# Mask sums, first taps, paired conditioning columns and free weight remainders in a two-layer diffusion step

## Chip, cores and metric

One core of one Trainium2 chip runs the whole program, one launch. The metric is device microseconds of a run, the median of the runs shown. PE is the matrix engine, DVE the vector engine, ACT the scalar engine, POOL the general engine, SP the queue that issues the transfers.

## What is computed

One step of a two-layer backbone over 128 prompt tokens and 512 sample tokens of width 2048. In each layer:

```python
h = rmsnorm(x, norm_pre[l]) * (1.0 + scale) + shift
(qa, ka, va, za, beta_raw, alpha_raw, cq, ckv, kpe, zb, xc, zc) = split_cols(h @ w_in[l])
oa, s_f, s_b = delta_branch(qa, ka, va, za, beta_raw, alpha_raw, conv_w[l], a_log[l],
                            dt_bias[l], o_norm_a[l], s0_f, s0_b)
ob = mla_attend(qn, qp, kn, kp, vb) * jax.nn.silu(zb)
oc = multiscale_pool(xc, w_pool[l], pool_scale[l]) * jax.nn.silu(zc)
y = jnp.concatenate([oa, ob, oc], axis=-1) @ w_out[l]
x = x + gate * rmsnorm(y, norm_post[l])
```

`scale`, `shift` and `gate` come from `silu(cond) @ w_ada[l] + b_ada[l]`, for two conditions. `delta_branch` has 8 heads: a convolution of 5 taps over q, k and v, then a gated delta rule in both directions, which needs `decay = exp(where(tri, gc_i - gc_j, -inf))` and the inverse of a triangular matrix for every block of 128 tokens.

## The kernel before

Layout. Tokens are five tiles of 128 (`NT`), held as two groups of 384 and 256 columns. A product in full precision is three products of rounded halves: `wsplit` (line 767) makes of four weight tiles a rounded half `hi` (a copy on ACT) and a remainder `lo` = raw - hi (a subtraction on POOL), each 128x512, into three buffers; `win_group` (line 783) multiplies them with the split activations, per weight tile three products over 384 and three over 256 columns. These are the projections of `w_in`; in the trace and the orders below they read `psum<-slabr`.

Order of the work. Nothing is issued in the order of the source. The class `Sched` records every operation, gives each a cost by `cost` (line 209), and `run` (line 350) plays engines, transfers and buffers forward; an operation goes to its engine when it is ready there, by priority (`later` shifts it). `either` (line 309) records an operation with a second form for another engine, and the engine that is idle first in this play takes it. `issue` (line 469) writes the result out, so each engine has a fixed order; line 499 issues everything, and all rows carry it. On the chip each engine follows its order, whatever the real times are.

Stages of a layer: `phase_a` makes the projections for gates and attention, the attention (`mla`), then for each of 8 heads `head_in` (projections of k, q, v and gate, with `conv_tile`, line 841) and `delta` (line 1182), then four pooling groups (`pool_group`); `phase_b` (line 1485) is the output projection. `head_in` of head h+1 is recorded ahead of `delta` of head h+1, so projections of the next heads and pooling groups stand between the small products of a scan and fill PE. In the first layer the conditioning columns of the second are worked in with `ada_cols` (line 1475): 16 beside the pooling groups, 16 beside the output projection.

A head, with the lines that the text speaks of:

- `conv_tile`: first tap `tensor_scalar` on DVE over 642 columns (line 849), four further taps on DVE (line 851).
- `delta`, lines 1188 to 1194: the decay table E, two directions of 128 x (5 x 128). A transfer fills it; per tile t one DVE step adds a per-partition scalar and the mask; one ACT exponential over 640 columns follows.
- key and query products, per tile three products over 256 columns from `kq` (hi and lo of k and q), into the one bank `pr`; four DVE steps multiply them with E (`slabV`/`slabW` as outputs) and free the bank for the next tile.
- the inversion: diagonal blocks go through DRAM into 40 rows, 31 pairs of DVE steps (`TENSOR_TENSOR slab<-slab 40x31` to `40x256` and back to `40x31`), a copy 40x1024, and through DRAM back.
- the scan: begins with 20 products 32x32 (`slab,slabW 32x32`) that need the landed inverse, then steps of 128x128 with DVE between them.

The DVE order mixes the inversion of head h+1 with the scan of head h.

`ada_cols`: a column block of 128 of `w_ada` (1 MB) lands in one of two buffers `ad2w`; 16 products into a bank, an ACT copy to `ao2`, a transpose into the same bank tag, a DVE reduction into `mcol`. `ad2w` lies over the buffers E, so it can be filled only when the last head has used them.

Of the kernel before, what the change touches and what calls it, by code (L numbers as in the profile page):

```python
# [18 lines left out]
NK = 16  # L19
# [4 lines left out]
NT = 5  # L24
# [477 lines left out]
class Body:  # L502
# [5 lines left out]
    def memory(self):  # L508
# [46 lines left out]
        put("S", SW - 128, [("ao2", 1, 128)], SW)  # L555
# [211 lines left out]
    def wsplit(self, raw, either=False):  # L767
        nc = self.nc
        n = cols(raw)
        hi = self.T("whi", [128, n], F32R)  # L770
        lo = self.T("wlo", [128, n], F32R)
        if either:
            self.copy(hi, raw)
            self.rest(lo, raw, hi)
        else:
            nc.scalar.activation(hi, raw, AF.Copy)
            nc.gpsimd.tensor_tensor(lo, raw, hi.bitcast(F32), op=ALU.subtract)
        return hi, lo
# [62 lines left out]
    def conv_tile(self, l, c0, ci, out):  # L841
# [7 lines left out]
        nc.vector.tensor_scalar(ac, cp[:, 0:KQW], w(0), None, op0=ALU.mult)  # L849
# [5 lines left out]
    def phase_a(self, l):  # L855
# [29 lines left out]
        for g in range(4):  # L885
            self.pool_group(l, g)
            if l == 0:
                self.ada_cols(l + 1, 16 + 4 * g, 20 + 4 * g, "ad2w", "pr2")
# [293 lines left out]
    def delta(self, l, h, ins):  # L1182
# [5 lines left out]
        for d in range(2):  # L1188
            e = self.T("E", [128, NT, 128])
            nc.sync.dma_start(e.rearrange("p t c -> p (t c)"), self.gcd[0].rearrange("(d h t) c -> d h (t c)", d=2, h=8)[d, h].partition_broadcast(128))  # L1190
            for t in range(NT):
                v.scalar_tensor_tensor(e[:, t], e[:, t], self.NGC[:, d * 8 + h, t:t + 1], self.mask[d], op0=ALU.add, op1=ALU.add)
            nc.scalar.activation(e, e, AF.Exp)
            E.append(e)
# [280 lines left out]
    def ada_cols(self, l, i0, i1, tag, pst):  # L1475
        nc, a = self.nc, self.a
        for i in range(i0, i1):
            w = self.T(tag, [128, NK, 128])
            nc.sync.dma_start(w, a["w_ada"][l, :, i * 128:(i + 1) * 128].rearrange("(k p) n -> p k n", p=128))
            p = self.ps(pst)  # L1480
            self.ada_rows(p, w, 0, True, True)
            with nc.later(-2):
                self.ada_sum(self.mcol[i // 16][:, :, i % 16:i % 16 + 1].rearrange("p v k -> p k v"), p, self.T("ao2", [128, 128]), pst)

    def phase_b(self, l):
# [53 lines left out]
        def columns(n):  # L1539
# [3 lines left out]
            for kc in range(NK // kn):  # L1543
# [6 lines left out]
                if n in (1, 2) and not last:  # L1550
                    i = 8 * (n - 1) + kc
                    self.ada_cols(l + 1, i, i + 1, "ad2w", "hp")
# [107 lines left out]
```

## Time and profile before

| | us |
|---|---|
| median of 3 runs | 2668.93 |
| lowest and highest run | 2667.51, 2675.01 |
| the profiled execution | 2681.82 |
| its span | 2680.0 |
| outside the span | 1.8 |

Engines by share of the span: PE 96%, DVE 58%, POOL 41%, ACT 36%. The chain that ended last is PE for 80%, transfers for 9%, DVE for 6%. The granted clock of PE over the span is 0.981 of full speed. Instructions in the orders: PE 17261, DVE 4096, ACT 2247, POOL 1103, SP 1042.

How to read it: a busy PE still has few places where it waits, so the places matter, not the shares. A wait is put down to the engine that ended it last; a wait on DVE inside the scans can be DVE's queue and not the one instruction.

### The profile page before, as it was taken

What the parts mean: (1) busy time and instruction counts of PE and PEld (TensorE: products, weight loads), DVE (VectorE), ACT (ScalarE), POOL (GpSimd) and SP (SyncE); (2) the same over time, 40 slices, a digit from 0 to 9 for tenths busy, and PEclk for the clock granted to TensorE, in tenths of its full rate; (3) what the DMA queues carried; (4) which work ended last, traced back from release to release, by engine and by line L of the source; (5) the groups of instructions that cost most, each with busy time, mean ns of one, the idle gap of its engine ahead of it and who ended that gap; (6) DMA issues with size and microseconds to landing.
All of it is one profiled execution on the core that took longest, in us unless ns stands there. A gap on an engine that the chain in (4) does not pass through costs nothing.

```text
span 2680.0 us, 53034 instructions
## 1 busy us (share of the span) xinstructions
PE 2559.6 (96%) x20553; PEld 2389.9 (89%) x20553; DVE 1565.9 (58%) x4094; ACT 966.6 (36%) x2635; POOL 1087.5 (41%) x1098
## 2 busy tenths in 40 slices
PE   4999999999999998999998999999999999989998
PEld 1689999999999998877797999999999999988888
DVE  3444456878887876330057254678778788655015
ACT  3233334334434333232247333343344333323222
POOL 0143224455444444353336432344545344446333
PEclk9999999999999999999998999999999899999999
DMA  9934443333443333896655434523343343335225
GB/s 313 329 96 116 134 118 113 98 90 89 98 98 96 80 94 88 228 284 181 184 161 165 132 93 125 146 77 97 92 102 93 83 98 91 87 82 185 95 75 189
DMA packets 541202, 347.98 MB, mean 130 GB/s; under 512 B 103826, under 2 KB 499734, under 8 KB 540310
## 3 DMA queue, kind: packets, MB, share of 16 engines
q1 hardware_dynamic: 540950, 344.59, 46.0%
q8 instruction: 162, 2.65, 0.4%
q14 instruction: 90, 0.74, 0.1%
HBM read 313.07 MB, written 31.46 MB: 129 GB/s over the span
## 4 chain that ended last, share of the span: by engine, by line
PE 80%; DMA 9%; DVE 6%; issue 2%; ACT 1%; SPq 1%; POOL 1%; DVEq 0%; ACTq 0%; POOLq 0%
PE psum L499 80%; DVE slab L499 5%; DMA slab<-d 3%; DMA slabW<-in_w_ada_dram 1%; SPq L499 1%; DMA slab<-in_w_in_dram 1%; DMA slab<-in_w_ada_dram 1%; ACT slab L499 1%; POOL slabr L499 1%; DMA slab<-in_w_out_dram 1%; DMA d<-slabV 1%; DVE slabV L499 0%; DMA slab<-in_x_prompt_dram 0%; DMA d<-slab 0%; ACT slabr L499 0%
## 5 line engine op out<-in xcount | busy, mean ns | idle before, releaser
L499 PE MATMUL psum<-slabr 128*128 128x384 f32 (+2 forms) x11760 | 2024.2, 325 | 11.3 <-DVE slabW L499 8.1
L499 PEld LDWEIGHTS psum<-slabr 128*128 128x128 f32 x11760 | 1784.5, 191 | 100.2 <-issue 23.9
L499 POOL TENSOR_TENSOR slabr<-slab,slabr 128x512 fp32r<-128x512 f32 (+3 forms) x706 | 834.4, 1190 | 1319.4 <-ACT slabr L499 1120.0
L499 ACT ACTIVATE slabr<-slab 128x512 fp32r<-128x512 f32 (+3 forms) x745 | 397.8, 546 | 903.9 <-PE psum L499 772.3
L499 PE MATMUL psum<-slab 128*128 128x128 f32 (+4 forms) x4375 | 442.5, 257 | 53.0 <-DVE slab L499 24.9
L499 DVE TENSOR_TENSOR slab<-slab 40x175 f32<-40x175 f32 (+19 forms) x1298 | 469.1, 373 | 33.0 <-DMA slab<-d 18.8
L499 ACT ACTIVATE slab<-psum 128x128 f32<-128x128 f32 (+7 forms) x839 | 278.6, 348 | 554.5 <-PE psum L499 434.8
L499 PEld LDWEIGHTS psum<-slab 128*128 128x128 f32 (+4 forms) x4375 | 356.0, 141 | 93.1 <-DVE slab L499 37.4
L499 DVE SCALAR_TENSOR_TENSOR slab<-slab 128x5 f32<-128x5 f32 (+7 forms) x618 | 360.0, 590 | 37.2 <-ACT slab L499 28.4
L499 DVE COPY slab<-psum 32x160 f32<-32x160 f32 (+9 forms) x214 | 85.1, 402 | 190.5 <-PE psum L499 159.2
L499 DVE TENSOR_REDUCE slab<-psum 128x2 f32<-128x8 f32 (+3 forms) x120 | 41.7, 350 | 235.3 <-PE psum L499 234.9
L499 DVE TENSOR_SCALAR slab<-slab 128x1 f32<-128x1 f32 (+8 forms) x408 | 152.8, 391 | 42.8 <-ACT slab L499 25.6
L499 DVE SCALAR_TENSOR_TENSOR slab<-psum,slab 128x128 f32<-128x128 f32 (+1 forms) x216 | 79.6, 377 | 96.6 <-PE psum L499 95.1
L499 ACT ACTIVATE slab<-slab 128x512 f32<-128x512 f32 (+4 forms) x195 | 103.6, 552 | 71.1 <-DVE slab L499 67.4
L499 DVE TENSOR_TENSOR slabr<-slab,slabr 128x384 fp32r<-128x384 f32 (+3 forms) x126 | 87.3, 698 | 45.4 <-PE psum L499 26.9
L499 DVE TENSOR_TENSOR slab<-psum,slab 128x512 f32<-128x512 f32 (+1 forms) x50 | 28.5, 584 | 142.3 <-PE psum L499 141.6
L499 PE MATMUL psum<-slab,slabW 32*32 32x32 f32 (+2 forms) x1216 | 82.3, 222 | 23.1 <-DMA slab<-d 21.3
L499 POOL TENSOR_SCALAR slab<-slabV,slab 128x128 f32<-128x128 f32 x128 | 66.3, 524 | 86.6 <-PE psum L499 85.2
L499 PEld LDWEIGHTS psum<-slab,slabW 32*32 32x32 f32 (+2 forms) x1216 | 67.4, 135 | 32.2 <-DMA slab<-d 24.0
L499 ACT ACTIVATE slab<-psum,slab 128x256 f32<-128x256 f32 (+2 forms) x91 | 58.5, 652 | 93.8 <-DVE slab L499 80.3
L499 DVE SCALAR_TENSOR_TENSOR slab<-slab,psum 128x128 f32<-128x128 f32 (+2 forms) x160 | 62.9, 397 | 43.4 <-PE psum L499 21.8
L499 POOL TENSOR_TENSOR slab<-slab 128x640 f32<-128x640 f32 (+5 forms) x46 | 66.3, 1442 | 40.0 <-ACT slab L499 29.9
(61 smaller groups left out, 1420.6 us busy)
## 6 DMA issues: line engine op xcount, KB each, us to landing
slab<-in_w_in_dram SPq DMA_DIRECT2D x186, 512.0 KB
slab<-in_w_ada_dram SPq DMA_DIRECT2D x32, 1024.0 KB
slabW<-in_w_ada_dram SPq DMA_DIRECT2D x32, 1024.0 KB
slab<-in_w_out_dram SPq DMA_DIRECT2D x64, 512.0 KB
slabW<-d SPq DMA_DIRECT2D x64, 320.0 KB
slabV<-in_w_ada_dram SPq DMA_DIRECT2D x32, 512.0 KB
slabW<-in_w_ada_dram SPq DMA_DIRECT2D x32, 512.0 KB
d<-slab SPq DMA_DIRECT2D x32, 320.0 KB
```

The lines of the kernel that those rows point to most:

```text
L499: op.inst = getattr(getattr(nc, op.eng), op.meth)(*[real(x) for x in op.a], **{n: real(x) for n, x in op.k.items()})
```

## The change

Four edits. (1) `delta`: one DVE addition of the mask over all 640 columns, and five ACT exponentials of 128 columns that take the per-partition scalar as bias. (2) `conv_tile`: the first tap may go to ACT. (3) `wsplit`: the remainder may go to POOL or DVE. (4) `ada_cols`: beside pooling groups and output projection two column blocks are loaded and multiplied into one bank, and evacuated together (a 256-column copy, two transposes, one reduction, one small copy into `mcol`); beside the output projection this is recorded at every second weight block.

```diff
@@ memory
-        put("S", SW - 128, [("ao2", 1, 128)], SW)
+        put("S", SW - 260, [("ao2", 1, 256), ("at4", 1, 4)], SW)
@@ wsplit
             nc.scalar.activation(hi, raw, AF.Copy)
-            nc.gpsimd.tensor_tensor(lo, raw, hi.bitcast(F32), op=ALU.subtract)
+            self.rest(lo, raw, hi)
@@ conv_tile
-        nc.vector.tensor_scalar(ac, cp[:, 0:KQW], w(0), None, op0=ALU.mult)
+        nc.either(("vector", "tensor_scalar", (ac, cp[:, 0:KQW], w(0), None), {"op0": ALU.mult}),
+                  ("scalar", "activation", (ac, cp[:, 0:KQW], AF.Copy), {"scale": w(0)}))
@@ phase_a
-                self.ada_cols(l + 1, 16 + 4 * g, 20 + 4 * g, "ad2w", "pr2")
+                self.ada_cols(l + 1, 16 + 4 * g, 20 + 4 * g, "ad2w", "pr2", 2)
@@ delta
+            v.tensor_tensor(e, e, self.mask[d].unsqueeze(1).to_broadcast([128, NT, 128]), op=ALU.add)
             for t in range(NT):
-                v.scalar_tensor_tensor(e[:, t], e[:, t], self.NGC[:, d * 8 + h, t:t + 1], self.mask[d], op0=ALU.add, op1=ALU.add)
-            nc.scalar.activation(e, e, AF.Exp)
+                nc.scalar.activation(e[:, t], e[:, t], AF.Exp, bias=self.NGC[:, d * 8 + h, t:t + 1])
@@ ada_cols
-    def ada_cols(self, l, i0, i1, tag, pst):
+    def ada_cols(self, l, i0, i1, tag, pst, m=1):
         nc, a = self.nc, self.a
-        for i in range(i0, i1):
-            w = self.T(tag, [128, NK, 128])
-            nc.sync.dma_start(w, a["w_ada"][l, :, i * 128:(i + 1) * 128].rearrange("(k p) n -> p k n", p=128))
+        for i in range(i0, i1, m):
+            ws = [self.T(tag, [128, NK, 128]) for _ in range(m)]
+            for j, w in enumerate(ws):
+                nc.sync.dma_start(w, a["w_ada"][l, :, (i + j) * 128:(i + j + 1) * 128].rearrange("(k p) n -> p k n", p=128))
             p = self.ps(pst)
-            self.ada_rows(p, w, 0, True, True)
+            for j, w in enumerate(ws):
+                with nc.later(-20 if j else 0):
+                    self.ada_rows(p[:, 128 * j:128 * j + 128], w, 0, True, True)
             with nc.later(-2):
-                self.ada_sum(self.mcol[i // 16][:, :, i % 16:i % 16 + 1].rearrange("p v k -> p k v"), p, self.T("ao2", [128, 128]), pst)
+                s = self.T("at4", [128, m, 2])
+                self.ada_sum(s, p, self.T("ao2", [128, 128 * m]), pst)
+                nc.vector.tensor_copy(self.mcol[i // 16][:, :, i % 16:i % 16 + m].rearrange("p v k -> p k v"), s)
@@ phase_b
-                if n in (1, 2) and not last:
+                if n in (1, 2) and kc % 2 and not last:
                     i = 8 * (n - 1) + kc
-                    self.ada_cols(l + 1, i, i + 1, "ad2w", "hp")
+                    self.ada_cols(l + 1, i - 1, i + 1, "ad2w", "hp", 2)
```

What the planner makes of it, over the whole program: PE keeps its 17261 instructions. DVE goes to 4231: 240 more remainders of 512 columns, 27 of 256, 3 of 384, 8 of 128 (all off POOL), 46 of the 48 first taps fewer (now on ACT), 160 mask steps fewer, 32 additions over 640 more, 48 small copies more. POOL goes from 1103 to 830, ACT to 2401 (160 exponentials of 128 for 32 of 640, 46 taps), SP stays at 1042. Of the remainders moved to DVE 24 lie between the first and the last head's inversion of each layer (0 to 5 a head), the others in attention, output projection and layer change. Both layers have the same order inside the heads.

PE ahead of the seventh head's scan, the first layer. `slabW 128x128` is a product of the sixth head's scan, `32x32 x20` begins the seventh's, `slabr` are projections and, over 256 columns, also the 15 key and query products of the eighth head. Before:

```order
L499 MATMUL psum<-slabr 128x384 x10
L499 MATMUL psum<-slab 128x128
L499 MATMUL psum<-slabr 128x384 x4
L499 MATMUL psum<-slab,slabW_3576 128x128
L499 MATMUL psum<-slabr 128x256 x30
L499 MATMUL psum<-slab,slabW_3576 32x32 x20
```

Of the change, the twelve rows up to the same 32x32 products (the `slabW 128x128` stands three rows further up, followed by `128x384 x10` and `128x256 x12`):

```order
L499 MATMUL psum<-slabr 128x384 x12
L499 MATMUL psum<-slabr 128x256 x12
L499 MATMUL psum<-slabr 128x384 x9
L499 MATMUL psum<-slabr 128x256 x3
L499 MATMUL psum<-slabr 128x384 x3
L499 MATMUL psum<-slabr 128x256 x12
L499 MATMUL psum<-slabr 128x384
L499 MATMUL psum<-slabr 128x256 x3
L499 MATMUL psum<-slabr 128x384 x11
L499 MATMUL psum<-slabr 128x256 x15
L499 MATMUL psum<-slabr 128x384 x5
L499 MATMUL psum<-slab,slabW_3582 32x32 x20
```

Between the two `slabW` rows there stood 30 `slabr` products; now there are 108, so projections stand between the key and query products.

PE late in the seventh head's scan, first layer (`slabV 128x512` and `slabV 128x128` behind it are products of a pooling group and the scan). Before:

```order
L499 MATMUL psum<-slab,slabV_3846 128x128
L499 MATMUL psum<-slabr 128x384 x8
L499 MATMUL psum<-slab,slabV_3846 128x512
L499 MATMUL psum<-slab 128x128 x4
L499 MATMUL psum<-slab,slabV_3846 128x128
L499 MATMUL psum<-slab 128x128
L499 MATMUL psum<-slab,slabW_3576 128x128
L499 MATMUL psum<-slabr 128x256 x16
L499 MATMUL psum<-slab,slabV_3846 128x512
```

Of the change:

```order
L499 MATMUL psum<-slab,slabV_3862 128x128
L499 MATMUL psum<-slabr 128x384 x28
L499 MATMUL psum<-slab,slabV_3862 128x512
L499 MATMUL psum<-slab 128x128 x4
L499 MATMUL psum<-slab,slabV_3862 128x128
L499 MATMUL psum<-slab 128x128
L499 MATMUL psum<-slab,slabW_3582 128x128
L499 MATMUL psum<-slabr 128x256 x5
L499 MATMUL psum<-slab,slabV_3862 128x512
```

Twenty projections more stand ahead of the first `slabV 128x512`, eleven fewer ahead of the second.

DVE at the start of the second head's inversion, first layer (`slab 40x...` are its steps). Before:

```order
L499 TENSOR_TENSOR slab<-slab 40x112
L499 COPY slab<-psum 64x5x64
L499 TENSOR_TENSOR slab<-slab 40x28x4
L499 SCALAR_TENSOR_TENSOR slabW_3576<-slabW_3576,slab 128x128
L499 TENSOR_TENSOR slab<-slab 40x135
L499 SCALAR_TENSOR_TENSOR slabW_3576<-slabW_3576,slab 128x128
L499 TENSOR_TENSOR slab<-slab 40x27x5
L499 SCALAR_TENSOR_TENSOR slabW_3576<-slabW_3576,slab 128x128
L499 TENSOR_TENSOR slab<-slab 40x156
L499 SCALAR_TENSOR_TENSOR slabW_3576<-slabW_3576,slab 128x128
```

Of the change:

```order
L499 TENSOR_TENSOR slabr<-slab,slabr 128x512
L499 TENSOR_SCALAR slab<-slab 128x642
L499 TENSOR_TENSOR slab<-slab 40x31
L499 TENSOR_TENSOR slabW_3582<-slabW_3582,slab 128x640
L499 TENSOR_TENSOR slab<-slab 40x31
L499 SCALAR_TENSOR_TENSOR slab<-slab 128x642
L499 COPY slab<-psum 128x128
L499 TENSOR_TENSOR slab<-slab 40x60
L499 SCALAR_TENSOR_TENSOR slab<-slab 128x642
```

The single mask steps between the inversion's steps have given way to one long addition, and a weight remainder (`slabr<-slab,slabr 128x512`) stands right ahead of the inversion.


## Rows read from the trace of the kernel before

**Rows 1.** the page, busy us, share of the span and instructions of each engine.

```profile
PE 2559.6 (96%) x20553; PEld 2389.9 (89%) x20553; DVE 1565.9 (58%) x4094; ACT 966.6 (36%) x2635; POOL 1087.5 (41%) x1098
```

**Rows 2.** windows: busy us (instructions) of PE, PEld, DVE, ACT, POOL; PEclk; DMA share; GB/s.

```profile
685.00:763.00 78.00, 76.86 (x653) 74.81 (x651) 64.84 (x167) 31.98 (x99) 37.50 (x35) 1.00 0.39 96
...
928.00:1007.00 79.00, 73.33 (x626) 71.61 (x627) 58.37 (x172) 27.41 (x90) 30.89 (x40) 0.89 0.33 84
1007.00:1072.00 65.00, 57.13 (x448) 52.76 (x446) 41.40 (x121) 19.99 (x65) 26.50 (x33) 0.92 0.35 88
```

**Rows 3.** windows, the same columns, output projection of layer 1 and of layer 2.

```profile
1190.00:1350.00 160.00, 159.98 (x1162) 127.66 (x1161) 18.35 (x38) 41.56 (x94) 54.76 (x47) 1.00 0.60 176
...
2450.00:2600.00 150.00, 150.00 (x663) 124.22 (x662) 25.36 (x37) 38.44 (x75) 67.20 (x54) 1.00 0.36 114
```

**Rows 4.** waits of PE, heads of layer 1 (500:1075): total us, times, longest us.

```profile
PE psum L499 <- DMA slab<-d: 10.4, 7, 2.4
PE psum L499 <- DVE slab L499: 7.9, 7, 2.9
PE psum L499 <- DVE slabW L499: 4.0, 2, 2.4
```

**Rows 5.** waits of PE, heads of layer 2 (1815:2390), the same columns.

```profile
PE psum L499 <- DMA slab<-d: 10.9, 7, 2.2
...
PE psum L499 <- DVE slabW L499: 4.1, 2, 2.4
```

**Rows 6.** windows, columns as in rows 2, four short stretches inside the heads.

```profile
927.00:940.00 13.00, 10.69 (x134) 10.01 (x134) 9.33 (x19) 3.53 (x12) 2.14 (x3) 0.61 0.37 73
994.00:1005.00 11.00, 6.98 (x36) 6.45 (x35) 7.00 (x26) 2.30 (x7) 2.12 (x5) 0.69 0.49 112
1047.00:1063.00 16.00, 9.12 (x34) 6.66 (x33) 13.32 (x44) 2.09 (x5) 4.12 (x7) 0.68 0.21 66
2077.00:2094.00 17.00, 15.33 (x173) 14.12 (x173) 10.49 (x26) 4.69 (x16) 2.54 (x4) 0.60 0.38 85
```

**Rows 7.** timeline of PE before the seventh scan, layer 2: start us, us, instructions, wait.

```profile
2295.43 10.07 PE L499 MATMUL psum<-slabr 128*128 128x384 f32 x65
...
2311.12 0.62 PE L499 MATMUL psum<-slabr 128*128 128x256 f32 x3 [2.40 <-DVE slabW L499]
2313.43 5.82 PE L499 MATMUL psum<-slabr 128*128 128x256 f32 x27 [1.69 <-DVE slabW L499]
```

**Rows 8.** timeline of PE before the eighth scan, layer 1, the same columns.

```profile
1050.91 1.12 PE L499 MATMUL psum<-slab,slabV 128*128 128x512 f32 x2 [2.90 <-DVE slab L499]
...
1059.02 3.75 PE L499 MATMUL psum<-slabr 128*128 128x256 f32 x16 [0.81 <-DVE slab L499]
```

**Rows 9.** groups by form, and timelines of DVE: a weight remainder on POOL and on DVE.

```profile
L499 POOL TENSOR_TENSOR slabr<-slab,slabr 128x512 fp32r<-128x512 f32 x499 | 704.1, 1412 | 1173.5 <-ACT slabr L499 1065.1 <-PE psum L499 58.7 <-ACT slab L499 35.3
...
1431.06 1.59 DVE L499 TENSOR_TENSOR slabr<-slab,slabr 128x512 fp32r<-128x512 f32 x1
...
1455.06 0.71 DVE L499 TENSOR_TENSOR slabr<-slab,slabr 128x512 fp32r<-128x512 f32 x1 [1.01 <-ACT slabr L499]
```

**Rows 10.** timelines of DVE: first tap, mask step, and additions over 640 columns.

```profile
582.76 1.41 DVE L499 TENSOR_SCALAR slab<-slab 128x642 f32<-128x642 f32 x1 [0.50 <-ACT slab L499]
...
599.37 0.54 DVE L499 TENSOR_SCALAR slab<-slab 128x642 f32<-128x642 f32 x1
...
2259.96 0.33 DVE L499 SCALAR_TENSOR_TENSOR slabW<-slabW,slab 128x128 f32<-128x128 f32 x1
...
168.70 1.80 DVE L499 TENSOR_TENSOR slabV<-slab,slabV 128x640 fp32r<-128x640 f32 x1
...
217.21 0.83 DVE L499 TENSOR_TENSOR slabV<-slab,slabV 128x640 fp32r<-128x640 f32 x1
```

**Rows 11.** groups by form of ACT: exponential over 640, and a scaled copy of 128.

```profile
L499 ACT ACTIVATE slabW<-slabW 128x640 f32<-128x640 f32 x32 | 23.4, 732 | 6.9 <-DVE slabW L499 6.7
...
L499 ACT ACTIVATE slab<-slab 128x128 f32<-128x128 f32 x64 | 20.4, 355 | 14.0 <-DVE slab L499 14.0
```

## The prediction, made before the changed kernel ran

> **What bounds the kernel now.** I read the page's engine line first. PE is busy for 2559.6 of 2680.0 us, DVE for 1565.9, ACT and POOL for less [rows 1]. PE's instructions are the same after the change, so all that can be won is PE's idle time and its time at the lower clock. The windows come next, to find where that lies. The output projections have no idle time: PE is busy for 159.98 of 160 us in the first layer and 150.00 of 150 in the second, at the full clock [rows 3]. Inside the heads a quiet stretch is nearly as full (76.86 of 78 us, granted clock 1.00), while the two stretches at the end of a layer's heads are not: 73.33 of 79 us at clock 0.89 and 57.13 of 65 us at 0.92 [rows 2]. Last I read the waits of PE over the eight heads of each layer. They say who ended the idle time: the transfer that brings the inverse back (`slab<-d`, 10.4 and 10.9 us, 7 times a layer, once a head), DVE results in `slab` (7.9 us), and the table E in `slabW` (4.0 and 4.1 us, twice a layer) [rows 4, 5]. So the start, the output projections and the layer change are not what this change can shorten by much; I allow 3 us for all of them.
>
> The sum is made against the profiled execution: span 2680.0 us and 1.8 us outside it, 2681.8 us. That execution is 12.9 us above the median of the runs, 2668.93 us; I apply the difference that I find to the median.
>
> **Part 1, the projections that stand elsewhere.** The waits for the table E lie at one place, the key and query products of the eighth head ahead of the seventh scan. In layer 2, PE runs 65 projections in 10.07 us, then stops for 2.40 us and 1.69 us, both for DVE's `slabW` [rows 7]: the 30 `slabr` products there stand together, and each bank of key and query products must be emptied by DVE before the next. In the stretch of layer 1 PE is busy 6.98 of 11 us at a clock of 0.69 of full speed [rows 6]. By its end PE has idled 4.0 us, and the clock costs more: 11 x 0.31 = 3.4 us of full-speed time are missing, which is 6.8 us run at 1.2 GHz instead of 2.4. I count some 1.6 of these 6.8 us as idle anyway, and half of the other 5.2 us as lost. Together 4.0 + 2.6 = 6.6 us a layer, 13.2 us in both.
>
> The change puts 108 products there instead of 30, of which 15 are the key and query products. The other 93 are projections at 10.07 / 65 = 0.155 us [rows 7], 14.4 us of work, against 15 x 0.155 = 2.3 us before. That covers a 4.0 us wait with the DVE steps behind it, so I take the whole 13.2 us as won. The projections come from other heads, so I counted the cost there. Between the heads' groups of 32x32 products, the number of projections changes by +9, -25, +17, -40, -1, +65 and -4, and by -53 ahead of the first group. At 0.155 us the largest loss is 40 x 0.155 = 6.2 us of filler out of a head that holds some 83 us of PE work. The other heads of the layer hold 78 to 85 us, and after the change 76 to 81. A head with 76.86 us of work in 78 showed no loss [rows 2], so I cost this at nothing; if the cover is too thin the loss is the difference to the DVE chain, some 2 us a head.
>
> **Part 2, the end of the heads.** Ahead of the eighth scan PE waits 2.90 us for a `slab` result and then again in front of 16 projections [rows 8]. The stretch has 9.12 of 16 us busy at clock 0.68, and DVE is busy for 13.32 of the same 16 us [rows 6]. Idle time is 6.9 us. The clock is missing 16 x 0.32 = 5.1 us, or 10.2 us at 1.2 GHz, of which some 4 are idle; half of the rest is 3.1 us. So about 10 us a layer are at stake. But this segment gets 4 projections fewer, not more, and its length is set by DVE, which is almost full here. Moving 20 projections ahead closes a gap and opens it further on, at the 32x32 products. The bounds are 0 and 10 us a layer; I take 1.5, near the lower one because of DVE's 13.32 of 16 us: 3 us.
>
> **Part 3, the waits for the landed inverse** (21.3 us in both layers [rows 4, 5], with a clock of 0.61 and 0.60 behind two of them: 13 x 0.39 = 5.1 us and 17 x 0.40 = 6.8 us [rows 6]). The chain behind them is DVE's inversion and the transfers; the change neither shortens it nor takes the 32x32 products away. I keep them as they are. The bound for a gain is half of the 21.3 us and most of the 11.9 us of clock, if DVE starts the inversion earlier; that is a rival below.
>
> **Part 4, what the engines get and lose.**
>
> DVE, per head: some 4 remainders of 512 columns more, at 0.71 us alone or 1.59 us beside POOL [rows 9]; 3 first taps fewer, at 0.54 or 1.41 us; 10 mask steps fewer, at 0.33 us; 2 additions over 640 columns more, at 0.83 or 1.80 us [rows 10]. At the short prices that is 2.84 - 1.62 - 3.3 + 1.66 = -0.4 us. If remainders and additions run at the long price and taps had the short one, it is 6.36 - 1.62 - 3.3 + 3.6 = +5.0 us; with taps at the long price too, +2.4 us. I take 0, between -0.4 and +2.4: DVE has 78 - 64.84 = 13 us idle in a head [rows 2], POOL loses 4 x 1.41 = 5.6 us a head [rows 9] and so is beside DVE less often, and the taps that go were among those that ran long. The bounds for the range are -0.4 and +5.0 us a head.
>
> ACT: 160 exponentials of 128 at 0.355 us (the scaled copy is the nearest row) for 32 of 640 at 0.732 us [rows 11], 56.8 - 23.4 = +33 us, and 46 taps over 642 columns at 0.73 us, that same row's mean, +34 us. That is 67 us over 16 heads, 4.2 us a head. ACT is busy 31.98 of 78 us in a head [rows 2], so 46 us of idle time cover it; nothing is charged. The first tile of E is ready after 0.83 + 0.355 = 1.2 us in place of 5 x 0.33 + 0.73 = 2.4 us, a small help that part 1 already holds. If the cover were gone, 4.2 us a head would be the cost.
>
> The paired columns: 32 loads of 1 MB are issued as 16 pairs, and a pair uses both buffers, so the second pair can load only when the first is multiplied. In the output projection PE has other products without a break and the transfer share is 0.60 [rows 3]; a late block moves its own products back, and nothing waits for them until the layer change. The cover there is the output projection's own products; should the weights `w_out` queue behind two blocks on SP, the cost would be the time of one block: at 176 GB/s [rows 3] 1 MB takes 6 us. I charge nothing, with bounds of -3 and +6 us.
>
> The remainder in the output projection: POOL is busy 54.76 of 160 us and 67.20 of 150 us, DVE 18.35 and 25.36 [rows 3]; either engine has room, nothing is gained.
>
> **The rule that speaks against it.** In the rows a remainder on DVE took 1.59 us with POOL working beside it and 0.71 us with POOL idle, and a first tap 1.41 and 0.54 us [rows 9, 10]. The Trainium skill, page "SBUF — State Buffer", section "Who interferes with whom", says that a VectorE instruction with two SBUF inputs and a GpSimd instruction that reads SBUF share a port pair and block each other for the whole instruction, whoever issues first. By that rule a remainder on VectorE buys no parallelism while GpSimd works, and the trace agrees with it, at 1.59 against 0.71 us; the sum by it would be rival C's.
>
> **The sum.** -13.2 (part 1) - 3 (part 2) + 0 (parts 3 and 4) = -16.2 us: 2681.8 to 2665.6 us in the profiled execution, and 2668.9 to **2653 us** in the median, 0.6% faster. For itself this case reaches from 2645 to 2661 us: half of part 1 or all of it and half of part 2's 20 us.
>
> **The rivals.**
>
> B, *the wait only moves*. DVE's and PE's orders are fixed before the run; each scan starts when its inverse has landed. If DVE's inversion of the eighth head sets that time, then what PE no longer loses at the key and query products it loses in front of the next 32x32 products. For it: DVE is busy 58.37 of 79 us there [rows 2], and the waits for `slab<-d` come once a head [rows 4, 5]. Against it: the 93 products are work that needs doing, and they leave other heads by 40 or fewer. Time: 2668.9 with 3 us for the small parts either way, and up to half of part 1: 2661 to 2677 us. That the remainder is free to choose does little is part of it: the choice is made when the order is built, and not by which engine is idle on the chip.
>
> C, *DVE becomes the bound inside the heads*. The remainders stand among the inversion's steps, as the order of DVE shows, with one right ahead of its first step, and so do the additions over 640 columns. Each long price (1.59, 1.80 us [rows 9, 10]) then delays the inverse, and PE waits for it 14 times already [rows 4, 5], with the clock falling behind the wait [rows 6]. At +2.5 us for each of 14 heads that is 35 us, less the 16 won: 2669 + 35 - 16 = 2688 us. It decides against the change from 16 / 14 = 1.2 us of net delay per head on. For it: those waits show that the inversion is the chain that ends last in each head. Against it: 13 us of idle time of DVE in a head, and POOL's lighter load.
>
> D, *more is won*. If the mask steps and taps that leave DVE's queue let the inversion start earlier, the waits of part 3 shrink: half of 21.3 us and half of the 11.9 us of clock, 16.6 us on top of the forecast, which gives 2636 us.
>
> **Chances.** The forecast 0.54, D 0.12, B 0.22, C 0.12. No change means within 0.3%, 8 us, about what a measurement of this kernel can tell. The forecast and D are faster (0.66), B is the same (0.22), C slower (0.12). The range for 8 in 10 is 2630 to 2674 us: all of the forecast and of D and most of B; C is left out with a small part of B.
>
> **What the changed profile would show.** Part 1 is right if PE's waits for DVE `slabW` are gone in the waits of the heads, and the stretch ahead of the seventh scan is full at a clock near 1.00; PE's idle time in that stretch would be under 1 us. Part 2 is right if the stretch before the eighth scan still idles some 5 to 7 us. Part 3 holds if the waits for `slab<-d` add up to 10 or 11 us a layer; 6 or less would be D, 20 or more would be B or C. In part 4 the groups by form would show DVE's remainders of 512 columns at a mean of 0.9 to 1.2 us, with DVE's busy time up by some 200 us (240 x 1.1 us for remainders, 32 additions at 0.83 to 1.80 us, less 160 x 0.33 us and 46 taps), ACT's up by some 70 us, POOL's down by 300 to 400 us. A mean above 1.4 us, or a clock below 0.9 over whole heads, would make the prediction wrong toward C. Output projections with idle time would mean that the pairs cost something after all.

## The result, and the profile after

| | before | changed | ratio (95% interval) |
|---|---|---|---|
| median beside the prediction, us (4 runs each) | 2671.97 | 2636.03 | 0.9864 (0.9846 to 0.9883) |
| again, in a later comparison (9 and 4 runs) | 2688.77 | 2641.60 | 0.982 (0.9802 to 0.9838) |
| the profiled execution's span | 2680.0 | 2640.6 | |

The change makes the kernel 1.4 to 1.8% faster, 36 and 47 us. The prediction was 2653 us; the time is inside its range and 17 us below its value. The two intervals do not overlap: the kernel before took 2672 to 2689 us from one comparison to another, the changed one 2636 and 2642. So effects below about 0.5% cannot be told across the experiments' groups below; where such a difference is named, it is a reading of two profiles and not more.

The page's engine line of the changed kernel, which answers to [rows 1]:

```profile
PE 2541.0 (96%) x20553; PEld 2380.4 (90%) x20553; DVE 1664.4 (63%) x4229; ACT 1026.8 (39%) x2789; POOL 739.7 (28%) x825
```

PE idles 2640.6 - 2541.0 = 99.6 us, before 120.4: 20.8 us less. It is also busy 18.6 us less for the same instructions; together that is the 39.4 us between the spans. The windows of the eight heads of each layer, from the first 32x32 products of its first head to those of its last (columns as in [rows 2]), say where. Of before:

```profile
523.00:1072.50 549.50, 528.26 (x4421) 514.19 (x4422) 429.54 (x1171) 209.31 (x655) 248.34 (x261) 0.97 0.36 93
1837.30:2386.90 549.60, 528.11 (x4421) 514.65 (x4421) 429.27 (x1171) 209.28 (x656) 250.40 (x261) 0.97 0.37 93
```

Of the changed kernel:

```profile
510.80:1045.90 535.10, 524.04 (x4442) 510.40 (x4442) 433.68 (x1150) 232.62 (x720) 207.66 (x233) 0.99 0.37 95
1805.90:2342.40 536.50, 525.33 (x4444) 512.01 (x4444) 432.48 (x1150) 232.25 (x720) 205.88 (x233) 0.99 0.37 94
```

Both stretches are 27.5 us shorter together (1099.1 to 1071.6 us), although 42 more projections (6.5 us at 0.155 us) stand in them. The idle time in them falls from 42.7 to 22.2 us, which is nearly the whole of PE's idle gain. The granted clock in them rises from 0.97 to 0.99, and PE is busy 7.0 us less (1056.4 to 1049.4 us) for 6.5 us more work: that is 13.5 of the 18.6 us of busy time. The rest of the span is 12 us shorter, of which 6.5 us are those 42 projections.

The waits of PE over the heads, first layer (500:1050) and second (1790:2345), answer to [rows 4, 5]:

```profile
PE psum L499 <- DMA slab<-d: 3.6, 5, 1.0
PE psum L499 <- DVE slab L499: 3.2, 3, 1.6
PE psum L499 <- ACT slab L499: 1.5, 1, 1.5
...
PE psum L499 <- DVE slabW L499: 0.5, 1, 0.5
```

```profile
PE psum L499 <- DMA slab<-d: 4.2, 5, 1.4
PE psum L499 <- DVE slab L499: 3.8, 5, 1.5
...
PE psum L499 <- DVE slabW L499: 0.5, 1, 0.5
```

All three kinds of wait have shrunk: the table E from 8.1 to 1.0 us, the landed inverse from 21.3 to 7.8 us. The four short stretches at the same places of the program answer to [rows 6]: the stretches ahead of the seventh and of the eighth head's scan, the one behind the sixth head's wait, and the one behind the fourth head's wait in layer 2.

```profile
974.00:985.00 11.00, 9.96 (x97) 9.46 (x97) 7.36 (x20) 3.37 (x8) 3.78 (x5) 1.00 0.72 116
1022.00:1040.00 18.00, 14.12 (x76) 12.08 (x75) 16.02 (x46) 4.65 (x23) 8.29 (x10) 0.88 0.30 85
908.00:920.00 12.00, 11.96 (x191) 11.13 (x192) 9.86 (x22) 5.49 (x14) 1.78 (x3) 1.00 0.44 128
...
2044.50:2061.50 17.00, 16.22 (x219) 15.11 (x218) 14.25 (x33) 8.39 (x26) 6.29 (x8) 1.00 0.40 104
```

Three of the four run at the full clock, where it was 0.60 to 0.69. The timeline of PE ahead of the seventh scan (start, us, instructions, wait) answers to [rows 7]:

```profile
967.39 13.85 PE L499 MATMUL psum<-slabr 128*128 128x384 f32 x93
981.74 2.31 PE L499 MATMUL psum<-slabr 128*128 128x256 f32 x15 [0.49 <-DVE slabW L499]
984.59 0.73 PE L499 MATMUL psum<-slab,slabW 32*32 32x32 f32 x40 [0.55 <-DMA slab<-d]
```

The 93 projections take 13.85 us (14.4 were reckoned), and 0.49 us of the 4.1 us of waiting is left. The groups by form answer to [rows 9 to 11]:

```profile
L499 DVE TENSOR_TENSOR slabr<-slab,slabr 128x512 fp32r<-128x512 f32 x253 | 179.2, 709 | 330.4 <-ACT slabr L499 317.7 <-PE psum L499 9.1 <-ACT slab L499 2.2
...
L499 DVE TENSOR_TENSOR slabW<-slabW,slab 128x640 f32<-128x640 f32 x32 | 28.0, 886 | 13.5 <-DMA slabW<-d 13.4
...
L499 POOL TENSOR_TENSOR slabr<-slab,slabr 128x512 fp32r<-128x512 f32 x259 | 372.6, 1441 | 689.8 <-ACT slabr L499 554.4 <-PE psum L499 50.0 <-DMA slabW<-in_w_ada_dram 49.9
...
L499 ACT ACTIVATE slabW<-slabW,slab 128x128 f32<-128x128 f32 x160 | 53.0, 396 | 6.5 <-DVE slabW L499 6.2
```

A remainder takes 709 ns on DVE and 1441 ns on POOL, and an addition over 640 columns 886 ns: nearly the short prices of [rows 9, 10], so the two engines hardly meet.

To compare runs I cut each head of the trace into three spans: from a head's 32x32 products to the first step of the next inversion (delay), from there to the copy 40x1024 (inversion), and from the copy to the next 32x32 products (round trip through DRAM). Fourteen such cuts, summed:

| | heads | delay | inversion | round trip | rest of span |
|---|---|---|---|---|---|
| before | 1099.1 | 179.0 | 763.1 | 157.0 | 1581.0 |
| changed | 1071.6 | 184.1 | 751.5 | 136.0 | 1569.0 |

The round trip is the largest part, 21 us. An example is the sixth head of layer 1, on SP (start, us, issue). Before, copy done at 915.9 us:

```profile
914.62 0.69 SPq L499 DMA_DIRECT2D d<-slab  x2
916.95 0.40 SPq L499 DMA_DIRECT2D slab<-in_w_in_dram  x1
917.44 0.82 SPq L499 DMA_DIRECT2D d<-slab  x2
918.31 0.98 SPq L499 DMA_DIRECT2D slab<-d  x2
919.39 0.34 SPq L499 DMA_DIRECT2D slab<-in_eyes_dram  x1
921.52 2.76 SPq L499 DMA_DIRECT2D slab<-d  x4
924.38 0.41 SPq L499 DMA_DIRECT2D slab<-in_w_in_dram  x1
924.84 2.57 SPq L499 DMA_DIRECT2D slab<-d  x3
```

After, copy done at 898.8 us:

```profile
898.87 0.65 SPq L499 DMA_DIRECT2D d<-slab  x2
899.88 0.40 SPq L499 DMA_DIRECT2D slab<-in_w_in_dram  x1
900.33 1.08 SPq L499 DMA_DIRECT2D slab<-d  x2
901.50 0.32 SPq L499 DMA_DIRECT2D slab<-in_eyes_dram  x1
901.91 4.00 SPq L499 DMA_DIRECT2D slab<-d  x7
```

Before, a weight load (`in_w_in`) stands ahead of the write of the inverse, which is issued at 917.44, 1.5 us after the copy, and another stands among the seven reads; the last read is issued at 927.4 us. After, one such load stands between the write and the reads, and the reads are out at 905.9. The trip takes 13.8 us before and 9.2 after. The two loads are only a part of these 4.6 us: by SP's waits the first waited 1.5 us for POOL's `slabr`, the second took 0.41 us, and SP waited 1.8 us for the write to land, which it does not do after. This trip is the longest of all; the sixth and the eighth heads of both layers make 15.8 of the 21 us.

### The profile page after: what moved, and what is told of

It reads as the page before. It is cut to its first block, busy times and chain, and to the rows that moved or that the text cites. A ratio compares the mean times of both kernels' runs of the same rounds, so it can differ in the third digit from the quotient of the medians.

```text
span 2640.6 us, 52982 instructions
## 1 busy us (share of the span) xinstructions
PE 2541.0 (96%) x20553; PEld 2380.4 (90%) x20553; DVE 1664.4 (63%) x4229; ACT 1026.8 (39%) x2789; POOL 739.7 (28%) x825
## 4 chain that ended last, share of the span: by engine, by line
PE 80%; DMA 6%; DVE 3%; ACT 2%; POOL 1%; issue 1%; SPq 1%; DVEq 0%; ACTq 0%
PE psum L499 80%; DVE slab L499 3%; DMA slab<-d 2%; DMA slab<-in_w_in_dram 1%; DMA slab<-in_w_ada_dram 1%; ACT slab L499 1%; POOL slabr L499 1%; DMA slabW<-in_w_ada_dram 1%; DMA d<-slab 1%; SPq L499 1%; ACT slabr L499 1%; ACT slabW L499 0%; DMA slab<-in_x_sample_dram 0%; DVE slabV L499 0%; DMA slabW<-d 0%
## 5 line engine op out<-in xcount | busy, mean ns | idle before, releaser
L499 POOL TENSOR_TENSOR slabr<-slab,slabr 128x512 fp32r<-128x512 f32 (+3 forms) x428 | 482.8, 1136 | 1200.3 <-ACT slabr L499 878.8
L499 DVE TENSOR_TENSOR slabr<-slab,slabr 128x512 fp32r<-128x512 f32 (+3 forms) x404 | 262.8, 654 | 416.1 <-ACT slabr L499 363.8
L499 DVE TENSOR_TENSOR slab<-slab 128x5 f32<-128x5 f32 (+20 forms) x1298 | 473.2, 376 | 19.2 <-DMA slab<-d 3.9
L499 ACT ACTIVATE slab<-psum 128x128 f32<-128x128 f32 (+6 forms) x823 | 276.1, 351 | 492.5 <-PE psum L499 384.7
L499 DVE SCALAR_TENSOR_TENSOR slab<-slab 128x5 f32<-128x5 f32 (+7 forms) x618 | 348.2, 572 | 42.9 <-ACT slab L499 33.9
L499 ACT ACTIVATE slab<-slab 128x642 f32<-128x642 f32 (+4 forms) x240 | 141.1, 603 | 62.3 <-DVE slab L499 55.7
L499 DVE TENSOR_SCALAR slab<-slab 128x1 f32<-128x1 f32 (+7 forms) x363 | 111.4, 326 | 29.0 <-ACT slabW L499 16.2
L499 DVE TENSOR_REDUCE slab<-psum 128x4 f32<-128x16 f32 (+3 forms) x104 | 39.5, 380 | 106.5 <-PE psum L499 105.3
L499 PE MATMUL psum<-slab,slabV 128*128 128x128 f32 (+1 forms) x352 | 72.4, 296 | 1.9 <-DVE slab L499 1.4
```

The costliest lines, as they stand in the source:

```text
L499: op.inst = getattr(getattr(nc, op.eng), op.meth)(*[real(x) for x in op.a], **{n: real(x) for n, x in op.k.items()})
```

## The experiments

**First group: order or work?** The planner turns any edit into a new order. These three kernels separate the two: the planner runs as before, and an operation is exchanged only when the finished order is written out. PE's order is then the same, instruction for instruction. The kernel before took 2683.6 us here, where the expectations reckoned with 2670; so the times that the expectations give are read 13.6 us higher.

`kept_masktap`, the order of before, with the new operations (in the loop that writes the order out; `whole`, `parts` and `tap` are marks set where the operations are recorded):

```diff
+            if hasattr(op, "whole"):
+                if op.whole:
+                    nc.vector.tensor_tensor(real(op.whole[0]), real(op.whole[0]), real(op.whole[1]), op=ALU.add)
+                continue
+            if hasattr(op, "parts"):
+                for x, y in op.parts:
+                    nc.scalar.activation(real(x), real(x), AF.Exp, bias=real(y))
+                continue
+            if hasattr(op, "tap"):
+                op.eng, op.meth, op.a, op.k = op.tap
```

> The orders of the kernel before are kept on every engine; only the operations are exchanged where they stand: the mask in one addition of 640 columns and five exponentials with bias, all first taps on ACT. Counted in DVE's order and priced by the mean durations of the two traces, DVE's work between first and last step of the 16 inversions goes from 788 to 736 us. Theory W (work): the heads gain because DVE has less to do inside the inversions, so the inverse lands earlier; then most of the 21.3 us of waits for it and some clock behind them go: 2645 us (2640 to 2655) where before is 2670. Theory O (order): the heads gain because the projections stand elsewhere, at the stall of the eighth head's key and query products and evenly over the heads; that is not in here, so 2662 to 2672 us.

Measured: 2682.5 us, ratio 0.9999 (0.9985 to 1.0012). Nothing is won. The waits of PE over the whole run of before:

```profile
PE psum L499 <- DMA slab<-d: 21.3, 14, 2.4
PE psum L499 <- ACT slab L499: 15.2, 8, 5.8
PE psum L499 <- DVE slabW L499: 8.1, 4, 2.4
```

Those of this run, and its window of the first layer's heads:

```profile
PE psum L509 <- DMA slab<-d: 19.6, 14, 2.4
...
PE psum L509 <- DVE slabW L509: 8.0, 4, 2.4
```

```profile
521.60:1065.90 544.30, 524.77 (x4421) 509.17 (x4421) 420.40 (x1107) 230.34 (x721) 236.59 (x261) 0.98 0.37 94
```

The waits are nearly those of before. DVE is busy 420.40 us instead of 429.54 in the window. Inside the 14 inversions it is busy 623.5 us instead of 638.2, but its idle time there rises from 124.8 to 138.0 us and the inversions last as long, 761.4 us. Most of that idle time ends with a result of PE (70.7 us before, 80.0 here) or of ACT: in a fixed order the inversion's steps stand behind instructions that wait for other engines, so the freed time becomes idle time. Theory W falls.

`held_masktap`, the order of the change, with the old mask and taps:

```diff
+            if hasattr(op, "steps"):
+                for x in op.steps:
+                    nc.vector.scalar_tensor_tensor(*[real(y) for y in x], op0=ALU.add, op1=ALU.add)
+                continue
+            if hasattr(op, "plain"):
+                op.k = {}
+            if hasattr(op, "tap"):
+                op.eng, op.meth, op.a, op.k = op.tap
```

> The mirror of it: the orders of the change are held on every engine, remainders stay where the change puts them, but the mask is made in five DVE steps and one exponential without bias per tile again, and all first taps are on DVE. DVE's priced work inside the inversions is 800 us, against 771 in the change and 788 before. W: the change's gain is gone, 2665 us (2658 to 2680). O: the order keeps its gain, 2636 to 2646 us.

Measured: 2658.2 us, 0.9912 (0.9896 to 0.9928), 25 us faster than before, at the upper end of O's span (2650 to 2660 us when read 13.6 us higher) and outside W's (2672 and more). In this order the old mask and taps cost the heads 10 to 12 us (1081.7 us against 1069.4 and 1071.6).

`held_pool`, the order of the change, weight remainders back on POOL:

```diff
+            if hasattr(op, "home"):
+                op.eng = op.home
```

> The orders of the change are held, but every weight remainder of 512 and 256 columns that stands on DVE goes back to POOL at its place. DVE's priced work inside the inversions falls from 771 to 746 us, POOL is again busy for about 1090 us. W: 25 us less work on DVE, so a gain on the change, 2625 us (2620 to 2632). O: 2632 to 2640 us, as the change. If the remainder's free choice itself is what pays (POOL too slow to feed the weights at a remainder's 1.41 us), it is slower than the change by 10 us or more, 2646 to 2665 us.

Measured: 2652.9 us, 0.989 (0.9872 to 0.9907), inside O's span (2646 to 2654 us when read 13.6 us higher) and above W's; against the change, whose ratio was 0.982 and 0.9864, it is 6 to 18 us slower. The third case, that the remainder's free choice itself pays, asked for 10 us or more and so for 2660 us and more: it holds in part. The split of the profile says where: heads 1065.8 us, 4 to 6 less than the change; rest 1580.1 us, 11 more. So in this order the remainder on DVE pays outside the heads, which O and W had not said; that it costs a little inside them is the reading of this one profile.

**Second group** (before 2688.8 us). The first run is the change itself, for comparison:

> The changed kernel itself, as the measure for the runs beside it: 0.986 of before, 34 to 40 us faster.

Measured: 0.982, as in the table above, and 47 us faster where 34 to 40 were expected. `held_allold` joins the exchanges of `held_masktap` and `held_pool`; of the four edits only the pairs stay:

> The orders of the change on every engine, but all operations of the heads and weights as before: mask in five DVE steps and one exponential without bias per tile, first taps on DVE, weight remainders on POOL. Theory O (the order pays): at least half of the gain stays, ratio to before 0.988 to 0.993, 18 to 32 us faster than before. Theory P (each part pays by the time that it takes off an engine): nothing is left but the pairs, 0.998 to 1.003.

Measured: 2677.6 us, 0.9956 (0.9942 to 0.9971), 11 us faster than before, a quarter of the change's 47 us. The order is worth something when only the pairs are left of the operations that it was planned for, but less than O expected and more than P. In its profile the heads last 1089.8 us and the rest 1585.7 us. Against `held_masktap` (1081.7 and 1570.1 us) the remainders on DVE win 16 us outside the heads and 8 us inside them, so that they cost time in the heads is not shown.

`only_mask` is edit (1) alone, `only_rest` edit (3) alone, as in the diff of the change, each with the order that the planner then makes:

> The mask edit alone, with the order that the planner makes of it. Projections between the groups of 32x32 products of a layer: 386, 458, 401, 445, 372, 402, 197 (before 412, 455, 401, 442, 400, 329, 243; change 421, 430, 418, 402, 399, 394, 239). O: the segment of the seventh head is filled now, the last one has 46 fewer, so some 10 us of gain: ratio 0.993 to 0.999. P: DVE's priced work inside the inversions falls from 788 to 752 us, the largest share of the change's gain: 0.988 to 0.992.

> The remainder edit alone. Projections between the groups of 32x32 products: 424, 449, 459, 362, 474, 289, 234. O: the segment of the seventh head has 40 fewer than before and 105 fewer than the change, so the stall ahead of its scan is longer: 10 to 27 us slower than before, ratio 1.003 to 1.010. P: POOL loses some 300 us of work and the weights are ready earlier, 0.994 to 0.998.

Measured: `only_mask` 2666.6 us, 0.9914 (0.9891 to 0.9937), outside O's span and inside P's. `only_rest` 2653.8 us, 0.9866 (0.9848 to 0.9884): O expected it slower and P expected 0.994 to 0.998; it is 35 us faster, so both miss. Its waits over the heads of layer 1:

```profile
PE psum L499 <- DVE slab L499: 7.3, 6, 2.2
PE psum L499 <- DVE slabW L499: 3.1, 2, 1.7
PE psum L499 <- DMA slab<-d: 1.8, 2, 0.9
```

The stall for E is still there, as O said, but the wait for the landed inverse is nearly gone (10.4 before). So an even spread of the projections is not what decides, and the counts per head do not foretell the time.

**Third group** (before 2682.2 us).

`held_mix` sends back to POOL only the remainders that stand among the steps of a layer's 8 x 62 = 496 inversion steps:

```diff
+            if op.eng == "vector" and op.meth == "tensor_tensor" and op.a[0].shape[0] == 40:
+                steps += 1
...
+            if hasattr(op, "home") and 0 < steps % 496:
+                op.eng = op.home
```

> The change with its orders, but the 54 weight remainders that stand on DVE between the first and the last step of a layer's inversions go back to POOL; all others stay on DVE. The profiles of the runs before, split into the heads (first to last group of 32x32 products of both layers) and the rest, gave heads 1069 to 1072 and rest 1569 to 1570 us for the change, heads 1066 and rest 1580 us for all remainders on POOL. If that split is real (theory S), this takes the better of both: heads about 1066, rest about 1570, 3 to 5 us faster than the change, ratio to before 0.981 to 0.985. If DVE's share in the heads is what feeds the weights (theory R), heads are 1072 or more and it is not faster than the change.

Measured: 2640.8 us, 0.984 (0.9816 to 0.9863); heads 1067.0, rest 1571.3 us. The split is as S said, within 1.3 us, and the heads, 2 to 5 us shorter than the change's, are too little to tell it from the change itself. No run beat the change clearly.

`only_tap` and `only_pair` are edits (2) and (4) alone:

> The tap edit alone: 38 of 48 first taps on ACT, with the order that the planner makes of it; projections between the groups of 32x32 products 430, 452, 399, 442, 345, 410, 197. If the edits add up (P), mask (0.9914) and remainder (0.9866) alone already exceed the change, so tap and pairs together cost 0.4 to 0.8%, and this is 1.000 to 1.006. If every new order wins the same waits once (theory U: the waits for the inverse go with nearly any other order), it is 0.988 to 0.996 by itself.

> The pairs alone, which take nothing off any engine inside the heads; the order inside the heads still comes out otherwise: 395, 461, 363, 472, 377, 357, 218. P: 0.998 to 1.006. U: 0.988 to 0.997.

Measured: 2655.7 us, 0.9896 (0.9873 to 0.9919), and 2660.8 us, 0.9911 (0.9887 to 0.9936). Theory U holds for both, P for neither. The four edits alone give 0.9, 1.0, 1.3 and 0.9%, together 4.1%, and joined 1.4 to 1.8%. The pairs take no instruction out of the heads at all, and still their heads last 1061.4 us, where 78 projections (12 us) have left them: a gain of some 26 us in the heads that only the order can have made; of the operations, only five remainders of 128 columns a layer went from DVE to POOL with it.

`replan` makes no edit of the change, but a belief of the planner:

```diff
-            return 0.15 + n * (2.1e-3 if meth == "tensor_tensor" else 1.6e-3)
+            return 0.15 + n * (2.46e-3 if meth == "tensor_tensor" else 1.6e-3)
```

> No edit of the change: the kernel before, whose planner believes a subtraction on POOL to take 2.46 ns a column in place of 2.1 (1.41 us for 512 columns, as the trace has it). Operations are the same but for some 30 halves and remainders that fall to another engine; only the order is new: 425, 459, 341, 439, 369, 378, 179. U: faster by 0.3 to 1.2%, ratio 0.988 to 0.997. If the edits' operations are what pays, 0.997 to 1.005.

Measured: 2697.1 us, 1.0049 (1.0032 to 1.0066), at the upper end of the other theory's span and slower. Its waits of PE:

```profile
PE psum L499 <- ACT slab L499: 35.8, 23, 6.3
PE psum L499 <- DVE slabW L499: 12.6, 8, 2.8
...
PE psum L499 <- DMA slab<-d: 4.4, 2, 2.4
```

Against the waits of before, shown above, those for the inverse went here too (21.3 to 4.4 us), and others took their place (ACT from 15.2 to 35.8 us). U in its simple form, that any other order wins, is wrong.

**Last run** (before 2682.1 us): the same belief in the changed kernel.

> The changed kernel, all four edits in, but planned with the same other belief as the run replan (2.46 ns a column for a subtraction on POOL). 31 fewer remainders of 512 columns are on DVE and 8 fewer taps on ACT; the order is new: projections between the groups of 32x32 products 465, 492, 344, 472, 380, 343, 142, as uneven as in replan. If the operations pay, whatever the order, the gain of the change stays: ratio to before 0.980 to 0.989. If the order that the change happened to get pays, most of it is gone: 0.992 to 1.005; the same belief cost the kernel before 0.5%.

Measured: 2672.5 us, 0.996 (0.9945 to 0.9974). Most of the gain is gone, as the second theory said; against `replan`, 1.0049, the edits still win 0.9%.

## Why the prediction was near, and where it was wrong

| planned with | operations of before | of the change |
|---|---|---|
| the order of before | 1 | 0.9999 (mask and taps only) |
| the order of the change | 0.9956 (the pairs stay) | 0.982 to 0.986 |
| a new order each, belief 2.46 | 1.0049 | 0.996 |

The range held the time only because it took in rival D: the span that the prediction gave for its own case, 2645 to 2661 us, did not hold the 2636 us.

*Part 1* was right as to the place and the mechanism. Idle time in the stretch fell from 4.02 to 1.04 us and its clock from 0.69 to 1.00; by the prediction's own reckoning that is 3.0 + 2.6 = 5.6 us a layer, 11.2 against the 13.2 forecast. `only_rest` shows that it is not needed for most of the gain.

*Part 2* was mis-sized: "I take 1.5, near the lower one", and its sign, 5 to 7 us of idle time left, did not come. In the stretch ahead of the eighth scan 3.9 of 18 us idle at clock 0.88 (before 6.9 of 16 at 0.68). That is 3.0 us of idle time, and the missing clock fell from 5.1 to 18 x 0.12 = 2.2 us, so some 5 us a layer by the prediction's way of counting, where 1.5 were taken. DVE is still almost full there, 16.02 of 18 us.

*Part 3* is the step that failed: "I keep them as they are". The waits for the landed inverse fell from 21.3 to 7.8 us, and the clock behind two of them came back to 1.00. I had looked at the length of DVE's chain and not at what stands on SP between its copy and the reads; the round trips lost 21 us and the inversions 12 us, while the delays ahead of them grew by 5. Parts 1 and 2 at their measured size (21 us) and the 13.5 us of these waits make 34.5 us; the heads won 34.0 (27.5 us shorter with 6.5 us more work). This sum is rough. The clock behind the two waits, 5.1 and 6.8 us by the prediction's count, is not in it, and neither is what other waits took back: the three items hold 25.5 us of idle time, and PE's idle time in the heads fell by 20.5 us. The other 5.4 of the 39.4 us between the profiles lie outside the heads.

*Part 4* took DVE's net work per head as 0, and that was near. With the means of the whole program it is 4 x 0.709 - 3 x 0.952 - 10 x 0.393 + 2 x 0.886 = -2.2 us. (0.952 and 0.393 us are the means of the old taps and mask steps in the trace of before.) Counted where they stand, in the heads' windows, these steps lose 0.7 us a head, and yet DVE is busy there 866.2 us after 858.8, 0.5 us a head more: other steps took longer, the copy 40x1024 for one 1375 ns on the mean after 1099, and no run says why. So DVE had no less to do in the heads. POOL's busy time fell by 348 us (300 to 400 forecast) and ACT's rose by 60 (70 forecast); DVE's rose by 98 only, not by 200, since the remainders took 709 ns and not 1.1 us. `kept_masktap` shows that freed DVE time by itself is worth nothing in the order of before. "I allow 3 us for all of them", of the stretches outside the heads, was too little: 5.4 us were won there, and the remainder's choice is worth 11 us in this order by `held_pool` and 16 by `held_allold` against `held_masktap`. Of the output projections the prediction was right, the pairs cost nothing there: they stay full, 159.70 of 160 us.

*Rival C* did not happen: of 253 remainders on DVE 202 run with POOL busy for less than 5% of their time, at 692 ns on the mean, and taking the 54 in the heads away made no difference that can be told from noise. One reading of [rows 9] was wrong: beside the remainder of 0.71 us POOL was not idle, since one of its subtractions began at 1455.35 us, while that remainder ran from 1455.06 to 1455.77. The 692 ns stand in its place as the price alone. The rule on the shared port pair in the Trainium skill, page "SBUF — State Buffer", section "Who interferes with whom", is not contradicted by that: the instructions seldom met here, and the 51 that did took 774 ns on the mean and 1528 ns at the longest.

*Rival D* gave the time, 2636 us, and the sign given for it was there, waits for `slab<-d` of 6 us a layer or less (3.6 and 4.2). Its reason did not: the inversions started no earlier, for the delays ahead of them grew by 5 us, and the same edits in the old order gave 0.9999. That its number is met is luck: its terms were 13.2, 3 and 16.6 us, of which the first two measured 11.2 and 10, and the kernel before was 3 us slower beside the change than the 2668.9 us that the sum began from. *Rival B* named the right danger, that orders are fixed before the run, with the wrong sign.

The cuts of the other profiles, made as in the table of the result, us:

| | heads | delay | inversion | round trip | rest of span |
|---|---|---|---|---|---|
| order of before, new mask and taps (`kept_masktap`) | 1094.7 | 174.8 | 761.4 | 158.5 | 1580.5 |
| order of the change, pairs alone (`held_allold`) | 1089.8 | 195.9 | 759.4 | 134.5 | 1585.7 |
| order of the change, pairs and remainders (`held_masktap`) | 1081.7 | 197.5 | 752.1 | 132.1 | 1570.1 |
| order of the change, pairs, new mask and taps (`held_pool`) | 1065.8 | 180.7 | 749.1 | 136.0 | 1580.1 |
| operations of before, belief 2.46 (`replan`) | 1089.7 | 155.3 | 791.4 | 143.0 | 1607.3 |

The round trips go with the order and not with the operations: 157 to 159 us in the order of before, 132 to 136 in the order of the change. They do not decide the time alone: in `held_allold` they are as short as in the change, but its delays are 17 us longer than before, and `replan` has short trips and is slower than before. What the new mask and taps add shows in the delays: in the order of the change they take 13 to 15 us off them, in the order of before 4.

What the runs show is that the operations and the order are worth little apart, as far as they were tried: the remainders in the order of before were not. The order with the pairs is worth 0.4%, mask and taps in the order of before nothing, all together 1.4 to 1.8%. Another belief of the planner makes the changed kernel 1.0 to 1.4% slower and the kernel before 0.5%. So part of the gain belongs to this one order and not to the edits. Which property of an order decides stays open: neither the spread of the projections nor DVE's work among the inversion's steps foretold the single edits. The SP queue was read in the trace and not tried by itself.

## What to carry to other kernels

Where a planner makes the order, an edit has two effects, its work and a new draw of the order, and the second may be the larger; hold the order and exchange the operations, then the reverse, before a gain is put down to an operation. Time that is freed on an engine in a fixed order can turn into idle time, as it did here in the order of before, unless the order is made anew for it. When PE waits for a value that travels through DRAM, read the issuing queue between the last copy and the reads too, and not only the engine that computes it.

## What was not expected of the hardware

The same kernel before had medians of 2672, 2684, 2689, 2682 and 2682 us in five comparisons, a spread of 0.6%, while the changed kernel had 2636 and 2642, 0.2%. The single runs of the kernel before spread as far within one comparison (2672.4 to 2688.2 us). A remainder of 512 columns costs 709 ns on DVE and 1441 ns on POOL, so DVE does it in half the time here.
